# A two-layer attention trunk: x resident behind the norm weights, and the distance table moved from VectorE to GpSimd

## The chip, the cores and the metric

The kernel runs on one core of one Trainium2 chip. The metric is the device time of one execution in microseconds (us); lower is better. A core has a matrix engine (TensorE, PE in the profile, with PEld for its weight loads), VectorE (DVE), ScalarE (ACT), GpSimd (POOL) and SyncE (SP), which here issues every DMA. Each engine works through its own queue in order, and waits on semaphores for what others produce. SBUF is the on-chip memory with 128 partitions; matmuls accumulate in banks of PSUM.

## The reference, cut to what matters

The model has two layers over 256 tokens of width 2048, in float32. Layer A is latent attention with 16 heads, layer B differential attention with 8 heads and a distance penalty.

```python
def rms_norm(x, gain):
    y = xf * lax.rsqrt(jnp.mean(xf * xf, axis=-1, keepdims=True) + EPS)
    return (y * gain)
...
def mla_layer(x, pos, ...):                        # layer A
    z = rms_norm(x, norm_g) @ w_in
    cq, ckv, k_pe, gate = jnp.split(z, ...)        # 512, 512, 64 and 2048 columns
    q = (rms_norm(cq, q_norm_g) @ w_q_up)...       # then heads, rotary part, softmax with a chunk mask
    return x + (o * jax.nn.silu(gate)) @ w_out
...
def diff_attend(q, k, v, pos, lam):                # layer B
    dist = jnp.abs(pi[:, :, None] - pos[:, None, :])
    sc = sc - slopes * dist
    sc = jnp.where(chunk_allowed(pi, pos), sc, -jnp.inf)
    p = jax.nn.softmax(sc, axis=-1)
    p_diff = p[:, :, 0] - lam * p[:, :, 1]
```

`lam` comes from two dot products of learned vectors: the exponential of the one, less the exponential of the other, plus a constant. `chunk_allowed` lets a token see its own chunk of 64 and all before it.

## The kernel before, in words

**Arithmetic.** Each product is made of three matmuls (`mm3`, lines 122 to 125): both operands are split into a high half, rounded to the matrix engine's format, and a low half, the remainder; high times high, high times low and low times high are summed. The low half of a weight tile (`wlo`) is made on DVE, from the raw tile and the high half (line 119); the high half (`whi`) is a cast on ACT (line 118; the very first piece is cast on DVE).

**Weights.** `stream` (line 105) loads one tile of weights from HBM (`raw`, four buffers) and splits it (`whi` and `wlo`, three buffers each). Every matmul weight of the kernel comes through it. A load of `raw` waits until the tile four back is split; a cast to `whi` waits until PE is done with the tile three back.

**The stage of the change.** x arrives feature-major (`xT`, 16 tiles of 128 features by 256 tokens). Line 163 runs a loop over k = 0 to 15. Step k loads one weight tile of 128 x 1088 (`wz[k]`, for k under 3 split in three pieces, for k = 0 loaded in three as well); scales tile k of x by its norm weight and splits it (`xh` on ACT, line 151, and `xl` on DVE, line 152); and runs 18 matmuls, three for each of three column blocks and two halves of the tokens, into six PSUM banks (`pg`, `pu`, `pa`). x is loaded one tile at a time for k = 0 and 1, then two at a time, through a tag of two buffers (`xs`, line 166). After each load's last step, ACT squares the raw x (lines 185 and 188) and POOL adds the squares up (`sqx`, line 189), for the mean square of each token. The norm weights (`gains_t`) are loaded behind the first piece of weights and the first tile of x (line 169). At k = 7 the positions and some small rows are loaded (lines 194 to 196).

Behind the loop in the program stand the tables (lines 199 to 283): rotary angles, sines and cosines (`ang`, `cs`, `ropc`, `rops`), the chunk mask `maskA`, the distance table `distB` (lines 272 to 275, on DVE: subtract, absolute value, add a very large number where the mask forbids, change the sign), and the two dot products for `lam` (`lamp`, `lams`, lines 279 and 281). Nothing in layer A uses `distB`; layer B reads it once per head (line 675, on POOL) and adds it to the scores. `posrf` and `posf` are the positions as floats, along the free axis and on the partitions.

Then follow the latents (`latents`, line 292: squares on ACT, scaling on DVE, and a reciprocal root on POOL), the heads of layer A with the gate's projection between them, its output projection, and layer B in the same manner.

**Order.** The program is written in the order above, and a scheduler orders each engine's queue by priority (earlier lines first) and readiness as it foresees it. So the table instructions stand between the steps of the loop on DVE, and the exponential of `lams` (line 619) stands on ACT among the casts of the last weight tiles. SP's DMA issues keep the program's order. The tag `junk` has one buffer: `lamp` and the throwaway outputs of the squares share it. The tag `gh` in the pool `big` is a buffer of 16 x 256 floats per partition; its first user before is `goh`, the attention output of layer A.

Of the kernel before, what the change touches and what calls it, by code (L numbers as in the profile page):

```python
# [9 lines left out]
F32 = mybir.dt.float32  # L10
# [3 lines left out]
AF = mybir.ActivationFunctionType  # L14
# [4 lines left out]
P = 128  # L19
# [35 lines left out]
def hybrid_kernel(ctx: ExitStack, tc: tile.TileContext, x, xT, pos, posc, rows, gains, wz, wgA, wqu, wkvu, woA, wB, woB, out):  # L55
# [18 lines left out]

# [1 line left out]
    gains_t = const.tile([P, 2 * KD + 14], F32, tag="gains", name="gains_t")  # L76
# [16 lines left out]

    # keep the tensor engine's clock up while the first operands arrive
    wsrc = const.tile([P, 512], BF16, tag="wsrc", name="wsrc")
# [4 lines left out]

# [1 line left out]
    state = {}  # L102
# [24 lines left out]
    def project(accs, lhs, blocks, w, c0, c1, nk):  # L127
        """accs[b][t] += lhs(k, t) . weights of block b, for the chunks c0..c1 of two contraction tiles each."""
        for c in range(c0, c1):
            ws = [stream(b[c], 2 * w) for b in blocks]  # L130
            for kk in range(2):
                k = 2 * c + kk
                for (hi, lo), acc in zip(ws, accs):
                    for t in range(NT):
                        xh, xl = lhs(k, t)
                        mm3(acc[t], xh, xl, hi[:, kk * w:(kk + 1) * w], lo[:, kk * w:(kk + 1) * w],
                            k == 0, k == nk - 1)
# [7 lines left out]

# [1 line left out]
    xh = big.tile([P, KD, S], F32R, tag="xh", name="xh")  # L147
# [11 lines left out]
    ZB = [(0, 384), (384, 384), (768, 320)]  # L159
    xt = [None]  # L160
    sqx = sm.tile([P, 2 * S], F32, tag="kn", name="sqx", bufs=1)
    XC = [0, 1] + list(range(2, KD + 1, 2))
    for k in range(KD):
        def load_x(k=k):
            n = XC[XC.index(k) + 1] - k
            xs = att.tile([P, n, S], F32, tag="gT", name="xs", padded_shape=[P, 4, S])
            nc.sync.dma_start(xs, xT[:, k:k + n, :])
            if k == 0:
                nc.sync.dma_start(gains_t, gains)
            xt[0] = (k, xs, n)  # L170

        if k in XC and k > 0:
            load_x()
        wh, wl = stream(wz[k], ZW, [c for c, _ in ZB] + [ZW] if k < KCUT else None, load_x if k == 0 else None)
        k0, xs, n = xt[0]
        split_gain(xh[:, k, :], xl[:, k, :], xs[:, k - k0, :], gA_t[:, k:k + 1])
        for b, (c0, w) in enumerate(ZB):
            for t in range(NT):
                sl = slice(t * P, (t + 1) * P)
                mm3(zacc[b][t][:, :w], xh[:, k, sl], xl[:, k, sl], wh[:, c0:c0 + w], wl[:, c0:c0 + w],  # L180
                    k == 0, k == KD - 1)
        if k == k0 + n - 1:
            w = n * S
            if k < 2:
                A.activation(sqx[:, k * S:(k + 1) * S], xs.rearrange("p a b -> p (a b)"), AF.Square)
            else:
                sq = sm.tile([P, w], F32, tag="sg", name="sq", bufs=2)
                A.activation(sq, xs.rearrange("p a b -> p (a b)"), AF.Square)
                G.tensor_tensor(sqx[:, :w], sqx[:, :w], sq, ALU.add)
        if k == KCONST:  # L190
            posc_t = const.tile([P, NT], I32, tag="posc", name="posc_t")
            prow = sm.tile([P, 2, S], I32, tag="e", name="prow", bufs=2)
            rows_t = sm.tile([P, HR + 2 * ROPE + 4 * HD], F32, tag="qn", name="rows_t", bufs=1)
            nc.sync.dma_start(posc_t, posc)
            nc.sync.dma_start(prow[:, 0, :], pos.partition_broadcast(P))
            nc.sync.dma_start(rows_t, rows.partition_broadcast(P))

    # mean square of each row of x, and its root's reciprocal
    r0 = const.tile([P, NT], F32, tag="r0", name="r0")
# [14 lines left out]

# [1 line left out]
    posr_t = prow[:, 0, :]  # L216
# [25 lines left out]
    A.activation(cos_, kk_, AF.Sin)  # L242
    # ropc[q|k]: cosines, rops: signed sines, both times the gain of the element they multiply
    V.tensor_scalar(gqkr_t[:, 1, :], gqkr_t[:, 1, :], math.sqrt(AQK), None, ALU.mult)
# [25 lines left out]
    for t in range(NT):  # L270
        V.tensor_scalar(maskA[:, t, :], chrf, chcf[:, t:t + 1], -MASK, ALU.is_gt, ALU.mult)
        V.tensor_scalar(distB[:, t, :], posrf, posf[:, t:t + 1], None, ALU.subtract)
        V.scalar_tensor_tensor(distB[:, t, :], distB[:, t, :], -1.0, distB[:, t, :], ALU.mult, ALU.max)
    V.scalar_tensor_tensor(distB, maskA, -MASK_DIST / MASK, distB, ALU.mult, ALU.add)
    V.tensor_scalar(distB, distB, -1.0, None, ALU.mult)

    # lambda, on every partition
    lamp = sm.tile([P, 2, HD], F32, tag="junk", name="lamp", bufs=1)
    V.tensor_tensor(lamp, lam_t[:, 0:2, :], lam_t[:, 2:4, :], ALU.mult)
    lams = const.tile([P, 2], F32, tag="lams", name="lams")  # L280
# [3 lines left out]

# [1 line left out]
    m16 = big.tile([P, 2, 2, 4, S], F32R, tag="m16", name="m16")  # L286
# [5 lines left out]
    def latents():  # L292
# [13 lines left out]
        for t in range(NT):  # L306
# [4 lines left out]
            cns.append(cn)  # L311
        # shared rotary key: its square sum, and its rotated form with the gain
        kp = sm.tile([P, NT, ROPE], F32, tag="kp", name="kp", bufs=1)
# [25 lines left out]

# [1 line left out]
    KC = KD // 2  # L341
# [26 lines left out]
    def k_up(hp):  # L368
        """keys, normalised, and values of two heads"""
        ka = pair(psu)  # L370
        project([ka], lat(1), [wkvu[hp]], 512, 0, 2, 4)
        kn = sm.tile([P, NT, 2, NOPE], F32, tag="kn", name="kn", bufs=1)
        rt = sm.tile([P, 2, NT, 2, ROPE], F32, tag="rt", name="rt", bufs=1)
        ss = sm.tile([P, 2, NT, 2], F32, tag="ssq", name="ss")
        f = sm.tile([P, 2, NT, 2], F32, tag="fq", name="fq")
        for t in range(NT):
            k3 = ka[t].rearrange("p (h d) -> p h d", h=2)
            junk = sm.tile([P, 512], F32, tag="junk", name="junk", bufs=1)
            for h in range(2):
                A.activation(junk[:, :NOPE], k3[:, h, :NOPE], AF.Square, accum_out=ss[:, 1, t, h:h + 1])  # L380
        V.tensor_tensor(ss[:, 1], ss[:, 1], bc(sskp, 2), ALU.add)
        rsqrt(f[:, 1].rearrange("p b c -> p (b c)"), ss[:, 1].rearrange("p b c -> p (b c)"))
        vh = att.tile([P, NT, 2, P], F32R, tag="vh", name="vh")
        vl = att.tile([P, NT, 2, P], F32R, tag="vl", name="vl")
        for t in range(NT):
            k3 = ka[t].rearrange("p (h d) -> p h d", h=2)
            V.tensor_tensor(kn[:, t], k3[:, :, :NOPE], bc(f[:, 1, t], NOPE), ALU.mult)
            split(vh[:, t], vl[:, t], k3[:, :, NOPE:])
        for t in range(NT):
            V.tensor_tensor(rt[:, 1, t], krope[:, t, :].unsqueeze(1).broadcast_to([P, 2, ROPE]),  # L390
                            bc(f[:, 1, t], ROPE), ALU.mult)
        state["k", hp] = (kn, rt, ss, f, vh, vl)

    def q_up(hp):
        """queries of two heads, not scaled: their norm enters with the scores"""
        kn, rt, ss, f, vh, vl = state["k", hp]
# [25 lines left out]
    def head_t(hp):  # L422
# [13 lines left out]
        for i in (1, 0):  # L436
            for t in range(NT):
                T.transpose(pt[:, i, t * P:(t + 1) * P], rt[:, i, t].rearrange("p h d -> p (h d)"), ident)
        # each head's rotary rows: q as [hi; lo], k's hi and lo twice over, so that every product has 128 rows
        q2 = att.tile([P, 2, S], F32R, tag="q2", name="q2")  # L440
# [116 lines left out]

# [1 line left out]
    x1 = big.tile([P, NT, D], F32, tag="m16", name="x1")  # L559
# [65 lines left out]

# [1 line left out]
    def qk_b(h, c0, c1):  # L627
# [131 lines left out]

# [1 line left out]
    def finish_b(n, t, c0, c1):  # L761
# [20 lines left out]
def _columns(w, width):  # L782
    """(K, N) -> (N / width, K / 256, 128, 2 * width): blocks of columns in chunks of two row tiles."""
    k, n = w.shape
    a = w.reshape(k // 256, 2, 128, n // width, width).transpose(3, 0, 2, 1, 4)
    return a.reshape(n // width, k // 256, 128, 2 * width)
# [46 lines left out]
```

## Time and profile before

| | us |
|---|---|
| median of three runs (lowest, highest) | 847.49 (846.46, 847.53) |
| span of the profiled execution, first to last instruction | 845.0 |
| what the median has above that span | 2.5 |
| PE busy in the span | 835.9 |
| DVE, ACT, POOL busy | 564.6, 488.0, 86.4 |

No time of the profiled execution other than its span is given. A profile row of a timeline has the start, the duration, the engine, the line of the kernel, the operation, output and inputs, the shape and the number of merged instructions; in brackets stands the idle time of that engine before it, and what ended it. A row of the waits has the instruction that waited, what it waited for, the total, the number of times and the longest. A row of windows has a stretch, its length, and the busy time and number of instructions of PE, PEld, DVE, ACT and POOL, then the granted clock, the DMA share and the rate. The granted clock of TensorE is 1.000 throughout. Shares of the whole span say little about the first 60 us, which hold everything the diff touches; they have to be read there.

### The profile page before, as it was taken

To read this page: it belongs to the slowest core of one execution; us is meant where nothing else is said; L and a number is where in the kernel's file an instruction comes from. 1 tells how busy PE (TensorE), PEld (TensorE's weight loads), DVE (VectorE), ACT (ScalarE), POOL (GpSimd) and SP (SyncE) were. 2 spreads that over 40 slices of the span, in tenths; PEclk is the share of its full clock that TensorE was granted. 3 is DMA by queue.
4 is the path that set the end of the run, shared out by engine and by line. 5 is a ranking of instruction groups with operands and counts; after the bars stand their busy time and mean duration, and the time that the engine had idled before them with its cause. 6 is when DMAs were issued, how large, how long until landed. Compare 5 with 4: busy or idle time off the path is not lost.

```text
span 845.0 us, 11706 instructions
## 1 busy us (share of the span) xinstructions
PE 835.9 (99%) x4187; PEld 714.5 (85%) x4187; DVE 564.6 (67%) x968; ACT 488.0 (58%) x995; POOL 86.4 (10%) x113
## 2 busy tenths in 40 slices
PE   8999999999999999999999999999999999999998
PEld 6988888889888888888888888888888888888886
DVE  6968678788787866555647565565756566565543
ACT  7656687677767656555555465555555564554331
POOL 2300221122202200000010010010001000000000
PEclk9999999999999999999999999999999999999999
DMA  8755544534444645555555555554555555455661
GB/s 268 256 197 162 166 147 146 176 116 162 144 144 149 248 154 180 180 186 177 185 175 174 175 175 175 175 175 150 193 181 175 175 175 171 168 184 198 219 211 70
DMA packets 42954, 148.59 MB, mean 176 GB/s; under 512 B 5008, under 2 KB 6032, under 8 KB 42640
## 3 DMA queue, kind: packets, MB, share of 16 engines
q1 hardware_dynamic: 42896, 147.84, 52.5%
q8 instruction: 33, 0.54, 0.3%
q14 instruction: 25, 0.20, 0.1%
HBM read 145.73 MB, written 2.10 MB: 175 GB/s over the span
## 4 chain that ended last, share of the span: by engine, by line
PE 94%; DVE 3%; DMA 1%; ACT 1%; issue 0%; SPq 0%; POOL 0%; DVEq 0%; ACTq 0%
PE pu L123 14%; PE pu L125 14%; PE pu L124 14%; PE pg L124 13%; PE pg L123 13%; PE pg L125 13%; DVE wlo L119 1%; PE ptb L651 1%; PE ptn L430 1%; PE ptp L484 1%; PE pa L124 1%; DMA raw<-in_wz 1%; PE pa L125 1%; PE pa L123 1%; DVE xl L152 1%; PE ps L462 0%
## 5 line engine op out<-in xcount | busy, mean ns | idle before, releaser
L119 DVE TENSOR_TENSOR wlo<-raw,whi 128x1024 fp32r<-128x1024 f32 (+4 forms) x278 | 328.6, 1191 | 189.8 <-ACT whi L118 189.5
L118 ACT CAST whi<-raw 128x1024 fp32r<-128x1024 f32 (+3 forms) x277 | 282.2, 1025 | 233.6 <-PE pg L125 102.6
L123 PE MATMUL pu<-whi,x1h 128*128 128x512 f32 x256 | 101.3, 396 | 0.0
L123 PE MATMUL pg<-whi,x1h 128*128 128x512 f32 x256 | 100.5, 392 | 0.0
L125 PE MATMUL pu<-whi,x1l 128*128 128x512 f32 x256 | 99.9, 390 | 0.0
L124 PE MATMUL pu<-wlo,x1h 128*128 128x512 f32 x256 | 99.8, 390 | 0.0
L124 PE MATMUL pg<-wlo,x1h 128*128 128x512 f32 x256 | 99.7, 390 | 0.0
L125 PE MATMUL pg<-whi,x1l 128*128 128x512 f32 x256 | 99.7, 389 | 0.0
L125 PEld LDWEIGHTS pu<-whi,x1l 128*128 128x128 f32 x256 | 48.1, 188 | 10.2
L125 PEld LDWEIGHTS pg<-whi,x1l 128*128 128x128 f32 x256 | 48.1, 188 | 10.1
L123 PEld LDWEIGHTS pg<-whi,x1h 128*128 128x128 f32 x256 | 48.1, 188 | 9.5
L124 PEld LDWEIGHTS pg<-wlo,x1h 128*128 128x128 f32 x256 | 48.1, 188 | 9.4
L124 PEld LDWEIGHTS pu<-wlo,x1h 128*128 128x128 f32 x256 | 48.2, 188 | 9.2
L123 PEld LDWEIGHTS pu<-whi,x1h 128*128 128x128 f32 x256 | 48.1, 188 | 9.2
L123 PE MATMUL pg<-whi,xh 128*128 128x512 f32 (+1 forms) x128 | 49.8, 391 | 1.9 <-ACT whi L118 1.3
L124 PE MATMUL pg<-wlo,xh 128*128 128x512 f32 (+1 forms) x128 | 48.7, 381 | 1.9 <-DVE wlo L119 1.9
L123 PE MATMUL pg<-whi,goh 128*128 128x512 f32 x128 | 50.5, 395 | 0.0
L123 PE MATMUL pu<-whi,goh 128*128 128x512 f32 x128 | 50.1, 392 | 0.0
L124 PE MATMUL pg<-wlo,goh 128*128 128x512 f32 x128 | 49.9, 390 | 0.0
L125 PE MATMUL pg<-whi,gol 128*128 128x512 f32 x128 | 49.9, 390 | 0.0
L124 PE MATMUL pu<-wlo,goh 128*128 128x512 f32 x128 | 49.9, 390 | 0.0
L125 PE MATMUL pu<-whi,gol 128*128 128x512 f32 x128 | 49.9, 389 | 0.0
(246 smaller groups left out, 1551.1 us busy)
## 6 DMA issues: line engine op xcount, KB each, us to landing
raw<-in_wB SPq DMA_DIRECT2D x128, 512.0 KB, 3.2
raw<-in_wgA SPq DMA_DIRECT2D x32, 512.0 KB, 3.5
raw<-in_woA SPq DMA_DIRECT2D x32, 512.0 KB, 3.3
raw<-in_woB SPq DMA_DIRECT2D x32, 512.0 KB, 3.2
raw<-in_wkvu SPq DMA_DIRECT2D x16, 512.0 KB, 4.3
raw<-in_wz SPq DMA_DIRECT2D x15, 544.0 KB, 5.7
raw<-in_wqu SPq DMA_DIRECT2D x16, 384.0 KB, 3.1
x<-in_x SPq DMA_DIRECT2D x1, 2048.0 KB, 10.0
```

The source lines that it names most:

```text
L118: (V.tensor_copy if after_first and a == 0 else A.copy)(hi[:, a:b], raw[:, a:b])
L119: V.tensor_tensor(lo[:, a:b], raw[:, a:b], f32(hi[:, a:b]), ALU.subtract)
L123: T.matmul(o, shi, mhi, start=start, stop=False)
L124: T.matmul(o, shi, mlo, start=False, stop=False)
L125: T.matmul(o, slo, mhi, start=False, stop=stop)
L152: V.scalar_tensor_tensor(lo, src, g, f32(hi), ALU.mult, ALU.subtract)
L430: T.transpose(pt[:, h, t * P:(t + 1) * P], src[:, t, h, :NOPE], ident)
L484: T.transpose(pt[:, c, t * P:(t + 1) * P], e[:, t, c * P:(c + 1) * P], ident)
L651: T.transpose(pt[:, m, t * P:(t + 1) * P], qk[:, t, 2 * i + m, :], ident)
```

## The change

Two parts; comments and blank lines aside, nothing else is edited.

The first keeps the whole of `xT` in one buffer, 16 KiB in each partition, in the tag `gh`. Each load writes its own part of it, at the same places in the program as before, so that no load waits for an earlier part to be used. The load of the norm weights is issued first of all.

The second makes `distB` and `lamp` on GpSimd: minus the absolute distance as min(d, 0) - max(d, 0) with a helper tile `ahead`, then the mask's share (`far`) added. That is nine instructions on POOL in place of seven on DVE. The sum of `lamp` (`lams`) stays on DVE.

```diff
-            xs = att.tile([P, n, S], F32, tag="gT", name="xs", padded_shape=[P, 4, S])
-            nc.sync.dma_start(xs, xT[:, k:k + n, :])
-            if k == 0:
-                nc.sync.dma_start(gains_t, gains)
...
+    xs = big.tile([P, KD, S], F32, tag="gh", name="xs")
...
+    def load_x(k):
+        n = XC[XC.index(k) + 1] - k
+        nc.sync.dma_start(xs[:, k:k + n, :], xT[:, k:k + n, :])
+
+    nc.sync.dma_start(gains_t, gains)
     for k in range(KD):
...
+        split_gain(xh[:, k, :], xl[:, k, :], xs[:, k, :], gA_t[:, k:k + 1])
...
     for t in range(NT):
         V.tensor_scalar(maskA[:, t, :], chrf, chcf[:, t:t + 1], -MASK, ALU.is_gt, ALU.mult)
-        V.tensor_scalar(distB[:, t, :], posrf, posf[:, t:t + 1], None, ALU.subtract)
-        V.scalar_tensor_tensor(distB[:, t, :], distB[:, t, :], -1.0, distB[:, t, :], ALU.mult, ALU.max)
-    V.scalar_tensor_tensor(distB, maskA, -MASK_DIST / MASK, distB, ALU.mult, ALU.add)
-    V.tensor_scalar(distB, distB, -1.0, None, ALU.mult)
+        ahead = sm.tile([P, S], F32, tag="junk", name="ahead", bufs=1)
+        G.tensor_scalar(ahead, posrf, posf[:, t:t + 1], 0.0, ALU.subtract, ALU.max)
+        G.tensor_scalar(distB[:, t, :], posrf, posf[:, t:t + 1], 0.0, ALU.subtract, ALU.min)
+        G.tensor_tensor(distB[:, t, :], distB[:, t, :], ahead, ALU.subtract)
+    far = sm.tile([P, NT * S], F32, tag="junk", name="far", bufs=1)
+    G.tensor_scalar(far, maskA.rearrange("p a b -> p (a b)"), MASK_DIST / MASK, 0.0, ALU.mult, ALU.add)
+    G.tensor_tensor(distB.rearrange("p a b -> p (a b)"), distB.rearrange("p a b -> p (a b)"), far, ALU.add)
...
-    V.tensor_tensor(lamp, lam_t[:, 0:2, :], lam_t[:, 2:4, :], ALU.mult)
+    G.tensor_tensor(lamp, lam_t[:, 0:2, :], lam_t[:, 2:4, :], ALU.mult)
```

More of the change, by code (lines that the diff above doesn't have):

```diff
@@ L159, in hybrid_kernel @@
     ZB = [(0, 384), (384, 384), (768, 320)]
-    xt = [None]
+    xs = big.tile([P, KD, S], F32, tag="gh", name="xs")
     sqx = sm.tile([P, 2 * S], F32, tag="kn", name="sqx", bufs=1)
     XC = [0, 1] + list(range(2, KD + 1, 2))
+    def load_x(k):
+        n = XC[XC.index(k) + 1] - k
+        nc.sync.dma_start(xs[:, k:k + n, :], xT[:, k:k + n, :])
+    nc.sync.dma_start(gains_t, gains)
     for k in range(KD):
-        def load_x(k=k):
-            n = XC[XC.index(k) + 1] - k
-            xs = att.tile([P, n, S], F32, tag="gT", name="xs", padded_shape=[P, 4, S])
-            nc.sync.dma_start(xs, xT[:, k:k + n, :])
-            if k == 0:
-                nc.sync.dma_start(gains_t, gains)
-            xt[0] = (k, xs, n)
         if k in XC and k > 0:
[L173 to L176, printed above, removed]
+            load_x(k)
+        wh, wl = stream(wz[k], ZW, [c for c, _ in ZB] + [ZW] if k < KCUT else None, (lambda: load_x(0)) if k == 0 else None)
+        split_gain(xh[:, k, :], xl[:, k, :], xs[:, k, :], gA_t[:, k:k + 1])
         for b, (c0, w) in enumerate(ZB):
@@ L181, in hybrid_kernel @@
                     k == 0, k == KD - 1)
-        if k == k0 + n - 1:
-            w = n * S
+        if k + 1 in XC:
+            k0 = XC[XC.index(k + 1) - 1]
+            src = xs[:, k0:k + 1, :].rearrange("p a b -> p (a b)")
+            w = (k + 1 - k0) * S
             if k < 2:
-                A.activation(sqx[:, k * S:(k + 1) * S], xs.rearrange("p a b -> p (a b)"), AF.Square)
+                A.activation(sqx[:, k * S:(k + 1) * S], src, AF.Square)
             else:
                 sq = sm.tile([P, w], F32, tag="sg", name="sq", bufs=2)
-                A.activation(sq, xs.rearrange("p a b -> p (a b)"), AF.Square)
+                A.activation(sq, src, AF.Square)
                 G.tensor_tensor(sqx[:, :w], sqx[:, :w], sq, ALU.add)
```

## The prediction

> **What bounds the kernel now.** I read the page's first two parts, then the waits of TensorE in the first 70 us, then the timelines of DVE, ACT, POOL and SP there. On the page:
>
> ```profile
> PE 835.9 (99%) x4187; PEld 714.5 (85%) x4187; DVE 564.6 (67%) x968; ACT 488.0 (58%) x995; POOL 86.4 (10%) x113
> ```
>
> TensorE (PE) is busy 99% of 845.0 us, so the change can only touch the few microseconds in which PE waits. The waits up to 70 us, which hold all that the diff touches, are:
>
> ```profile
> PE pg L124 <- DVE wlo L119: 1.9, 2, 1.2
> PE pg L123 <- ACT whi L118: 1.3, 1, 1.3
> PE pg L123 <- ACT xh L151: 0.7, 1, 0.7
> ```
>
> That is 3.9 us, 0.46% of the span, and the prize can't be larger. The timeline of PE places them (start, duration, engine, line, tile, and in brackets the idle time before and what ended it):
>
> ```profile
> 9.50 0.62 PE L123 MATMUL pg<-whi,xh 128*128 128x384 f32 x2 [1.26 <-ACT whi L118]
> 13.99 0.44 PE L124 MATMUL pg<-wlo,xh 128*128 128x384 f32 x1 [0.72 <-DVE wlo L119]
> 43.86 0.34 PE L123 MATMUL pg<-whi,xh 128*128 128x384 f32 x1
> 45.38 0.44 PE L124 MATMUL pg<-wlo,xh 128*128 128x384 f32 x1 [1.18 <-DVE wlo L119]
> 45.66 0.33 PE L125 MATMUL pg<-whi,xl 128*128 128x384 f32 x1
> 45.83 0.34 PE L123 MATMUL pg<-whi,xh 128*128 128x384 f32 x1
> ```
>
> The first two belong to the start (k = 1 and k = 2 of the sixteen steps that multiply x by `wz`), the last to step 12. The start is the business of the first half of the change, step 12 of the second. At step 12, PE waits for the low half of the weights, `wlo`, and DVE made it late. I number that instruction by its step, wlo12; it is the first row here, and the others show what DVE did since it was last level with its suppliers:
>
> ```profile
> 44.04 1.28 DVE L119 TENSOR_TENSOR wlo<-raw,whi 128x1088 fp32r<-128x1088 f32 x1
> 24.18 1.29 DVE L119 TENSOR_TENSOR wlo<-raw,whi 128x1088 fp32r<-128x1088 f32 x1 [0.23 <-ACT whi L118]
> 32.00:40.00 8.00, 8.00 (x50) 8.00 (x49) 8.00 (x21) 5.83 (x11) 3.32 (x2) 1.00 0.76 239
> ```
>
> At 24.18 DVE still waited for ACT, so it was level. From then on it never idles (the window 32 to 40: 8.00 of 8.00 us in the third number), and 20 us later PE stands still for it. So in this stretch each microsecond added to DVE's queue is one of PE's, and each taken away is one saved until the wait is used up.
>
> **The start: x and the norm weights.** Now x goes through two small buffers, and SP issues its queue in the order of the program. So a load of x that waits for a buffer holds up the weights behind it:
>
> ```profile
> SPq L116 <- DVE wlo L119: 33.8, 16, 6.4
> SPq L167 <- DVE xl L152: 9.1, 6, 2.5
> 3.52 0.43 SPq L116 DMA_DIRECT2D raw<-in_wz  x1
> 5.48 0.33 SPq L167 DMA_DIRECT2D xs<-in_xT  x1
> 5.86 0.91 SPq L116 DMA_DIRECT2D raw<-in_wz  x2
> ```
>
> With one resident buffer there is nothing to wait for: x for k = 2 goes out at about 4.0 instead of 5.48, the weights of k = 2 and 3 from about 4.4 instead of 5.86, 1.5 us earlier. Most of the 9.1 us isn't worth anything, because the weight loads behind the later x loads wait for their own buffers too (33.8 us of SP's waits are for `wlo`). Putting the norm weights ahead moves `raw` and x of k = 0 by one issue each (0.47 us in this queue) and lets ACT start k = 0 sooner; PE then runs into the load of the weights of k = 1, which is seventh in the queue before and after. So I cost the reordering at nothing; its cover is the 1.26 us wait at 9.50, and without it one issue, 0.47 us, could be lost.
>
> What the earlier x buys shows on ACT and DVE:
>
> ```profile
> 10.72 0.91 ACT L151 ACTIVATE xh<-xs,gains_t 128x256 fp32r<-128x256 f32 x2 [0.50 <-DMA xs<-in_xT]
> 11.54 0.62 ACT L188 ACTIVATE sq<-xs 128x512 f32<-128x512 f32 x1
> 12.27 1.29 ACT L118 CAST whi<-raw 128x384 fp32r<-128x384 f32 x3
> 12.24 1.28 POOL L189 TENSOR_TENSOR sqx<-sqx,sq 128x512 f32<-128x512 f32 x1 [10.95 <-ACT sq L188]
> 12.81 3.32 DVE L119 TENSOR_TENSOR wlo<-raw,whi 128x384 fp32r<-128x384 f32 x4 [0.66 <-ACT whi L118]
> ```
>
> ACT waits 0.50 us for x and, after the square, 0.11 (12.16 to 12.27) for the weights. Both go, 0.6 us. POOL's add moves with them and still stands in front of the first low half of k = 2, so PE's wait at 13.99 shrinks by 0.6 and isn't gone. The ends: all of the wait (0.72, and 0.28 that PE idled just before it), 1.0, if the cast comes ahead of the square; or 0.4 lost, if more loads in flight, or the norm weights ahead, bring the weights of k = 1 later. I take a gain of 0.6, from ACT's rows.
>
> **The distance table.** DVE loses these (minimum, median, maximum in ns; the last row is the sort of POOL instruction that takes over):
>
> ```profile
> L272 DVE TENSOR_SCALAR distB<-rowf,posf x2: 341/342/344, 29.0 to 34.8; 128x256 f32<-128x256 f32 x2
> L273 DVE SCALAR_TENSOR_TENSOR distB<-distB x2: 414/415/416, 29.4 to 42.8; 128x256 f32<-128x256 f32 x2
> L274 DVE SCALAR_TENSOR_TENSOR distB<-maskA,distB x1: 677/677/677, 43.4 to 43.4; 128x512 f32<-128x512 f32 x1
> L279 DVE TENSOR_TENSOR lamp<-rows_t x1: 412/412/412, 35.1 to 35.1; 128x256 f32<-128x256 f32 x1
> L675 POOL TENSOR_SCALAR bias<-distB x8: 620/1457/1533, 267.6 to 647.9; 128x512 f32<-128x512 f32 x8
> ```
>
> Ahead of wlo12 that is 2 x 0.34 + 2 x 0.41 + 0.68 + 0.41 = 2.6 us; consecutive DVE instructions overlap by some 0.08, so six of them free 2.1 us of the queue. (L275 goes too, but it stands behind wlo12.)
>
> POOL gains nine instructions: four tensor_scalar on 256 elements, two tensor_tensor on 256, `far` (tensor_scalar on 512), an add on 512 and `lamp` (tensor_tensor on 256). Two rows price the tensor_tensor forms:
>
> ```profile
> L416 POOL TENSOR_TENSOR rt<-rt,r x8: 739/741/1586, 100.1 to 285.1; 128x256 f32<-128x256 f32 x8
> L189 POOL TENSOR_TENSOR sqx<-sqx,sq x7: 1282/1426/2436, 12.2 to 40.6; 128x512 f32<-128x512 f32 x7
> ```
>
> 256 elements take 0.74, 512 take 1.28. A tensor_scalar on 512 takes 0.62 undisturbed; on 256 it lies between half of that and all of it, and I take 0.40. Together 4 x 0.40 + 2 x 0.74 + 0.62 + 1.28 + 0.74 = 5.7 us. POOL has the time (3.32 us busy in the 8 us above). The question is whether DVE runs on meanwhile. It doesn't:
>
> ```profile
> 9.48 1.43 DVE L119 TENSOR_TENSOR wlo<-raw,whi 128x384 fp32r<-128x384 f32 x3 [1.41 <-ACT whi L118]
> 26.09 0.29 DVE L267 CAST rowf<-prow 128x256 f32<-128x256 int32 x1
> 26.21 1.43 POOL L189 TENSOR_TENSOR sqx<-sqx,sq 128x512 f32<-128x512 f32 x1 [4.69 <-ACT sq L188]
> 26.39 1.53 DVE L152 SCALAR_TENSOR_TENSOR xl<-xs,gains_t,xh 128x256 fp32r<-128x256 f32 x1
> 27.95 0.47 DVE L152 SCALAR_TENSOR_TENSOR xl<-xs,gains_t,xh 128x256 fp32r<-128x256 f32 x1
> ```
>
> The same DVE instruction takes 1.53 beside POOL's add and 0.47 without it; it ends 0.28 after POOL (27.64 to 27.92). POOL's add of 1.28 costs DVE 1.06. `wlo` suffers the same way: three short ones and a long one would have taken 1.43 and 1.28 less the overlap of 0.08, so 2.6, and took 3.32 from 12.81. So moving work to POOL doesn't take it out of DVE's way.
>
> How much do nine cost? If 0.22 of each is free (1.28 less 1.06), 5.7 less 9 x 0.22 = 3.7 us. If the free part is a share (1.06 of 1.28, 83%), 4.7. If nothing is free, 5.7. If they all fall where DVE doesn't want what POOL holds, 0; a gain below that is excluded, since POOL's instructions can't speed DVE up. I take 3.7: the add's row is the nearest, and a fixed start and end per instruction is what it shows. They come in time to count: the last of their first inputs (`posrf`, the cast at 26.09) exists at 26.4, and 5.7 us of POOL fit well before 44.
>
> The Trainium skill (SBUF — State Buffer, section "Who interferes with whom") has the rule that speaks against the change: DVE's second port pair is shared with GpSimd, and whichever instruction comes first holds it "for the whole instruction". The row gives 1.06 of 1.28, a little less. By the rule to the letter the term is 5.7, the second rival's time; by the row 3.7.
>
> Queues that gain a wait: `lams` (L281, DVE) now waits for POOL's last new instruction, and behind it on DVE stand wlo12 and the rest; ACT's exponential waits for `lams`, and behind that stand two casts of weights:
>
> ```profile
> 43.12 0.41 DVE L281 TENSOR_REDUCE lams<-lamp 128x2 f32<-128x256 f32 x1
> 43.56 0.20 ACT L619 ACTIVATE lams<-lams 128x2 f32<-128x2 f32 x1 [1.84 <-DVE lams L281]
> 43.67 2.08 ACT L118 CAST whi<-raw 128x1088 fp32r<-128x1088 f32 x2
> 46.98 1.29 DVE L119 TENSOR_TENSOR wlo<-raw,whi 128x1088 fp32r<-128x1088 f32 x1
> ```
>
> ACT waits there already, 1.84 us. Its next cast ends at 44.7 and DVE uses it at 46.98, so 2.2 us of cover; POOL's chain should be over by about 40. I cost this at nothing. POOL's next work after the sixteen steps comes at 58:
>
> ```profile
> 58.19 0.72 POOL L92 TENSOR_TENSOR r<-msx,nhalf 128x2 f32<-128x2 f32 x1 [16.09 <-DVE msx L208]
> ```
>
> It has idled 16 us by then, so it isn't held up. The users of `distB` start at 267.6.
>
> **The sum.** Against the profiled span of 845.0: start -0.6; freed on DVE -2.1; lost by DVE to POOL +3.7; together +1.0, so 846.0, PE's wait at step 12 growing from 1.2 to about 2.8. The median of the runs, 847.49, stands 2.5 above the span; the same shift gives 848.5. A change within 0.2%, 1.7 us, can't be told from none here, so "the same" is 845.8 to 849.2.
>
> **The rivals.** (1) Relief: the new work falls into moments when DVE wants nothing that POOL holds, or the order on DVE comes out so that the low halves go first. Then step 12's wait is gone (1.35: the matmul after the one at 43.86 should have started 0.17 later, as the rows at 45.66 and 45.83 do, not 1.52), and with the start -1.9: 845.6. For it: POOL is idle most of the stretch. Against: both the long weights and the short x instruction were held. It decides where DVE loses less than 2.1 - 1.35 = 0.8 us. (2) The port is held for the whole of each instruction, or DVE stands in order behind `lams` while POOL finishes: 5.7 - 2.1 - 0.6 = +3.0, 850.5. It turns the sign beyond doubt where DVE loses more than 2.1 + 0.6 + 1.7 = 4.4. For it: the nine follow one another, and each DVE instruction between them may meet a fresh one. (3) The start gains nothing because the loads share the same DMA engines: 3.7 - 2.1 = +1.6, 849.1, or above with the 0.4. (4) Loss and relief cancel: about 847.
>
> **How the numbers follow.** My forecast has 0.46 (0.36 of it within 0.2%, 0.10 above, since its own range, DVE losing 3.2 to 4.7, is 848.0 to 849.5), relief 0.19, full hold 0.23, no gain at the start 0.07 (half of it above), cancelling 0.05. Faster 0.19; same 0.36 + 0.03 + 0.05 = 0.44; slower 0.10 + 0.23 + 0.04 = 0.37. The low end is the relief with 0.3 more at the start, 845.3; the high end the full hold with the start's gain lost, 851.0.
>
> **What would show it.** Right: `xs` issues back to back with no wait on `xl`; PE's wait at k = 2 about 0.6 shorter, at k = 1 unchanged; nine POOL instructions between about 25 and 42, beside them L152 and L119 rows of 0.7 to 2 us; the wait of PE on `wlo` at step 11 or 12 at 2 to 3 us; nothing new after 60 us. Wrong: undisturbed L152 rows of 0.47 beside the new POOL instructions, or no wait at step 12 (relief); ACT idle for `lams` by more than 4 us (the queue); `raw` of k = 1 landing after 9.2 (the start).

## The result, and the profile after

| | before | after |
|---|---|---|
| median of five runs, us (lowest, highest) | 847.49 (846.46, 847.55) | 853.64 (852.78, 854.29) |
| ratio of the times (95% interval) | | 1.0076 (1.0064, 1.0088) |
| span of the profiled execution, us | 845.0 | 851.0 |

The change makes the kernel 6.2 us slower, 0.76%. That is 5.1 us above the forecast and 2.6 above the end of the range. From the page of the changed kernel:

```profile
PE 838.1 (98%) x4187; PEld 716.5 (84%) x4187; DVE 562.0 (66%) x961; ACT 490.7 (58%) x997; POOL 95.0 (11%) x122
```

POOL has its nine instructions more and DVE seven fewer, as the diff says. TensorE's waits of the changed kernel up to 75 us (its warm-up and a row of 0.3 us are left out); the last row is from 75 to 320 us, where the kernel before has no wait on `vl`:

```profile
PE pg L124 <- DVE wlo L119: 5.7, 2, 4.8
PE pg L123 <- ACT whi L118: 0.6, 1, 0.6
...
PE pu L123 <- DVE vl L156: 1.0, 1, 1.0
```

One wait has grown to 4.8 us, where the longest was 1.3. The timeline of PE in the changed kernel (start, duration, and in brackets the idle time and what ended it):

```profile
9.22 0.61 PE L123 MATMUL pg<-whi,xh 128*128 128x384 f32 x2 [0.63 <-ACT whi L118]
13.75 0.44 PE L124 MATMUL pg<-wlo,xh 128*128 128x384 f32 x1 [0.91 <-DVE wlo L119]
...
34.52 0.34 PE L123 MATMUL pg<-whi,xh 128*128 128x384 f32 x1
39.69 0.69 PE L124 MATMUL pg<-wlo,xh 128*128 128x384 f32 x1 [4.84 <-DVE wlo L119]
40.18 0.52 PE L125 MATMUL pg<-whi,xl 128*128 128x384 f32 x1
40.50 0.52 PE L123 MATMUL pg<-whi,xh 128*128 128x384 f32 x1
...
44.02 0.34 PE L123 MATMUL pg<-whi,xh 128*128 128x384 f32 x1
...
121.24 0.41 PE L123 MATMUL pu<-whi,m 128*128 128x384 f32 x1 [1.00 <-DVE vl L156]
```

The wait isn't at step 12 but at step 9, and behind it the matmuls start 0.32 us apart where 0.17 is usual. The windows of the changed kernel show why; the granted clock is the third number from the right:

```profile
40.00:41.00 1.00, 1.00 (x4) 1.00 (x4) 0.93 (x5) 0.42 (x3) 0.00 (x0) 0.50 0.53 65
41.00:42.00 1.00, 1.00 (x5) 1.00 (x4) 0.93 (x5) 1.00 (x3) 0.00 (x0) 0.50 0.72 270
42.00:43.00 1.00, 1.00 (x5) 1.00 (x5) 1.00 (x5) 1.00 (x4) 0.00 (x0) 0.57 0.99 392
```

After standing still, TensorE was granted half its clock for some three microseconds. The seventeen matmuls from the end of the wait, 39.69, to the next step, 44.02, took 4.33 us. The kernel before took 2.91 us for the same ones behind its wait, from 45.38 to the next step, which starts here:

```profile
48.29 0.34 PE L123 MATMUL pg<-whi,xh 128*128 128x384 f32 x1
```

So some 1.4 us are lost on top of the wait. What DVE was doing, in its timeline of the changed kernel:

```profile
26.66 0.61 DVE L152 SCALAR_TENSOR_TENSOR xl<-xs,gains_t,xh 128x256 fp32r<-128x256 f32 x1
...
29.33 1.28 DVE L119 TENSOR_TENSOR wlo<-raw,whi 128x1088 fp32r<-128x1088 f32 x1
30.53 0.76 DVE L234 SCALAR_TENSOR_TENSOR ang<-kh__596,ang 128x64 f32<-128x64 f32 x1
37.30 0.42 DVE L285 TENSOR_REDUCE lams<-lamp 128x2 f32<-128x256 f32 x1 [6.00 <-POOL lamp L283]
37.63 2.00 DVE L119 TENSOR_TENSOR wlo<-raw,whi 128x1088 fp32r<-128x1088 f32 x1
```

DVE, which never idled in this stretch before, stood 6.00 us for `lamp`, with the low half of step 9 directly behind it. In the kernel before `lams` stood at 43.12, shortly ahead of the low half of step 12; in the new program the scheduler put it ahead of step 9's. (The first row is used further down.) POOL's timeline of the changed kernel shows what `lamp` waited for:

```profile
26.24 1.44 POOL L274 TENSOR_SCALAR ahead<-rowf,posf 128x256 f32<-128x256 f32 x1 [5.09 <-DVE kk__595 L228]
27.66 2.33 POOL L275 TENSOR_SCALAR distB<-rowf,posf 128x256 f32<-128x256 f32 x2
29.97 1.25 POOL L276 TENSOR_TENSOR distB<-distB,ahead 128x256 f32<-128x256 f32 x1
31.17 1.29 POOL L189 TENSOR_TENSOR sqx<-sqx,sq 128x512 f32<-128x512 f32 x1
32.44 1.15 POOL L274 TENSOR_SCALAR ahead<-rowf,posf 128x256 f32<-128x256 f32 x1
33.67 0.74 POOL L276 TENSOR_TENSOR distB<-distB,ahead 128x256 f32<-128x256 f32 x1
34.50 0.62 POOL L278 TENSOR_SCALAR far<-maskA 128x512 f32<-128x512 f32 x1
35.20 1.26 POOL L279 TENSOR_TENSOR distB<-distB,far 128x512 f32<-128x512 f32 x1
36.54 0.72 POOL L283 TENSOR_TENSOR lamp<-rows_t 128x256 f32<-128x256 f32 x1
37.22 1.26 POOL L189 TENSOR_TENSOR sqx<-sqx,sq 128x512 f32<-128x512 f32 x1
```

`lamp` needs nothing of the table, but it is last of the nine on an engine that works in order. The nine take 1.44 + 2.33 + 1.25 + 1.15 + 0.74 + 0.62 + 1.26 + 0.72 = 9.5 us, not 5.7. (The expectations of two runs below put the new work at 8.7.) ACT's exponential then stood 5.10 us for `lams`:

```profile
37.75 0.20 ACT L623 ACTIVATE lams<-lams 128x2 f32<-128x2 f32 x1 [5.10 <-DVE lams L285]
```

The account, from the profiled executions: the wait 4.84 - 1.18 = +3.7, the halved clock +1.4, the new wait for `vl` +1.0, the first 14 us -0.24 (13.75 against 13.99): 5.9 of the 6.0 us by which the span grew. The rest is spread over small gaps and was not assigned. The profiled execution is the shortest of the five, 852.78 us, with a mean granted clock of 0.998. Three of the others had 0.995 and took 853.64 to 854.29 us, so the clock's share in the median is probably larger; there is no trace of them.

### The profile page after: what moved, and what is told of

Read it like the earlier page. It is cut to its first block, busy times and chain, and to the rows that moved or that the text cites. A ratio compares the mean times of both kernels' runs of the same rounds, so it can differ in the third digit from the quotient of the medians.

```text
span 851.0 us, 11698 instructions
## 1 busy us (share of the span) xinstructions
PE 838.1 (98%) x4187; PEld 716.5 (84%) x4187; DVE 562.0 (66%) x961; ACT 490.7 (58%) x997; POOL 95.0 (11%) x122
## 4 chain that ended last, share of the span: by engine, by line
PE 93%; DVE 2%; POOL 1%; ACT 1%; DMA 1%; issue 0%; SPq 0%; DVEq 0%; ACTq 0%; POOLq 0%
PE pu L123 14%; PE pu L125 13%; PE pu L124 13%; PE pg L124 13%; PE pg L125 13%; PE pg L123 13%; DVE wlo L119 1%; PE pa L124 1%; PE pa L125 1%; PE ptb L655 1%; PE ptp L488 1%; PE pa L123 1%; DMA xs<-in_xT 1%; PE ptn L434 1%; ACT whi L118 1%; PE psb L125 0%
```

## The experiments

Two theories stood against each other: the loss is the queue's (DVE waits in order behind POOL, and the clock halves for it), or it is the port's (DVE can't run beside POOL). Each ratio is against the kernel before on the same chip; that kernel's medians were 847.23, 846.79 and 847.10 us in the three sessions.

**The parts alone.** `e3_x_only` is the kernel before with the diff's first part, `e4_table_only` with its second.

> The first part alone: x in one resident buffer behind the norm weights, all tables on DVE as before. Theories Q and P agree: PE's wait at k = 2 ends 0.2 to 0.6 us earlier and nothing else changes, 846.9 to 847.3. Theory X (the first part is the cause): 852 or more.

> The second part alone: x loaded through two small buffers as before, distance table and lamp on GpSimd. Theories Q and P: 853 to 854.5, with DVE waiting about 6 us for lamp (Q) or with stretched DVE rows and no such wait (P). Theory X: 847 to 848.

Measured: x alone 846.94 us, ratio 0.9995 (0.9985 to 1.0004), which can't be told from no change; the table alone 853.24, ratio 1.0069 (1.0053 to 1.0084). The second has the same two waits as the whole change, for `wlo` 4.8 us at the longest and for `vl` 1.0. So the loss is the table part's.

**The wait for `lamp`.** `e1_lamp_dve` makes `lamp` on DVE again and leaves the table on POOL; `e2_lamp_first` leaves `lamp` on POOL and puts it ahead of the table.

```diff
e1:
-    G.tensor_tensor(lamp, lam_t[:, 0:2, :], lam_t[:, 2:4, :], ALU.mult)
+    V.tensor_tensor(lamp, lam_t[:, 0:2, :], lam_t[:, 2:4, :], ALU.mult)
e2, ahead of the loop over t that makes the table:
+    lamp = sm.tile([P, 2, HD], F32, tag="junk", name="lamp", bufs=1)
+    G.tensor_tensor(lamp, lam_t[:, 0:2, :], lam_t[:, 2:4, :], ALU.mult)
```

> The changed kernel with one edit: lamp is made on DVE again, the distance table stays on GpSimd. In the changed kernel DVE stands 6.00 us for lamp behind GpSimd's chain and PE 4.84 us behind DVE. Theory Q (the in-order wait for lamp is the cost): that wait goes, PE's wait near step 9 goes with it, 846.5 to 848. Theory P (GpSimd's instructions hold DVE's port, the forecast's term): lamp is only 0.72 of 8.7 us of new GpSimd work, so the time stays at 852 to 853.5.

> The changed kernel with one edit: lamp stays on GpSimd but is written ahead of the distance table, so that it stands first in GpSimd's chain. The work on each engine is the same as in the changed kernel. Theory Q: lams finds lamp ready or waits under 1.5 us, 846.5 to 848.5. Theory P: the same GpSimd work in the same stretch, 852 to 854.

Measured: e1 853.34, ratio 1.0065 (1.0051 to 1.0080); e2 851.71, ratio 1.0043 (1.0028 to 1.0059). In e1 the wait hadn't gone at all. DVE's timeline of e1:

```profile
37.76 1.47 DVE L283 TENSOR_TENSOR lamp<-rows_t 128x256 f32<-128x256 f32 x1 [5.21 <-POOL distB L279]
```

DVE now waits for POOL's add of `far` instead. `lamp`, `ahead` and `far` share the one buffer of the tag `junk`, and `lamp` may not write there until `far` has been read: the same queue, through a buffer. e1 therefore tells nothing of the port.

In e2 the wait for `lamp` is gone, but 3.6 us (by the ratio) to 4.5 us (851.71 against that session's 847.23) are still lost, which is in neither theory's range. Timelines of POOL and DVE in e2:

```profile
37.89 5.14 POOL L189 TENSOR_TENSOR sqx<-sqx,sq 128x512 f32<-128x512 f32 x3
39.00 4.18 DVE L254 SCALAR_TENSOR_TENSOR rops<-rows_t,cs 128x32 f32<-128x32 f32 x8
```

Three adds of squares, which arrive one by one in the kernel before, stand piled up behind the table and now run in a row. Beside them eight small DVE instructions take 4.18 us; undisturbed (in e11, below) they take 0.90. PE waits 3.4 us for low halves in e2, in four pieces. This looks like the port of the prediction, at work through adds that the kernel had all along; `e6_pool_late` below gives the comparison that shows it.

**The same with a buffer of its own.** `e5_lamp_own` is e1 with `lamp` in the tag `r2`, so that nothing on DVE waits for POOL.

```diff
-    lamp = sm.tile([P, 2, HD], F32, tag="junk", name="lamp", bufs=1)
-    G.tensor_tensor(lamp, lam_t[:, 0:2, :], lam_t[:, 2:4, :], ALU.mult)
+    lamp = sm.tile([P, 2, HD], F32, tag="r2", name="lamp", bufs=1)
+    V.tensor_tensor(lamp, lam_t[:, 0:2, :], lam_t[:, 2:4, :], ALU.mult)
```

> The run with lamp on DVE still stood 5.21 us, now for the release of the one buffer that lamp shares with GpSimd's helper tiles. Here lamp is on DVE in a buffer of its own, so DVE waits for nothing of GpSimd's chain. Theory Q alone (the wait in DVE's queue is the whole cost): 847 to 848. Theory Q and P together (the wait, or else the hold on DVE's port and the squares queued up behind the chain on GpSimd, as in the run with lamp first): no wait for GpSimd on DVE, but stretched DVE rows, 850 to 852.

Measured: 850.61, ratio 1.0044 (1.0030 to 1.0057). Timelines of POOL and DVE in e5:

```profile
38.13 4.97 POOL L189 TENSOR_TENSOR sqx<-sqx,sq 128x512 f32<-128x512 f32 x3
38.30 2.27 DVE L119 TENSOR_TENSOR wlo<-raw,whi 128x1088 fp32r<-128x1088 f32 x1
40.49 3.07 DVE L254 SCALAR_TENSOR_TENSOR rops<-rows_t,cs 128x32 f32<-128x32 f32 x8
```

The longest waits of PE in e5, up to 75 us and behind it:

```profile
PE pg L124 <- DVE wlo L119: 3.1, 2, 2.2
PE pu L123 <- DVE vl L156: 1.0, 1, 1.0
```

And one of e5's windows:

```profile
42.00:43.00 1.00, 1.00 (x5) 1.00 (x4) 1.00 (x1) 0.00 (x0) 1.00 (x1) 0.50 0.88 344
```

With no wait of DVE for POOL the table still costs 3.7 us (0.0044 of 847), as the two theories together expected. In the profiled execution PE waits 1.0 longer than before in one piece (2.2 against 1.2), loses some 1.5 to three microseconds of halved clock (4.46 us from the end of the wait, 40.62, to the next step, 45.08, against the 2.91 above), and has the late wait for `vl`, 1.0. As time the clock's part isn't shown: three of the five executions had a mean granted clock of 1.000 and took 850.08, 850.17 and 850.98 us, the two with 0.998 took 850.61 and 850.77. So the theory that the queue is all of it has fallen: part of what it cost is lost to the held port instead once it is gone.

**The price of the operation.** POOL's tensor_scalar on 256 elements took 1.1 to 1.4 us, and `far`, on 512, 0.62. `e8_immediate` replaces the operand `posf` by the constant 0 (its table leaves out the query's position); `e11_mult_add` also makes the operations a multiplication by 1 and an addition of 0 (its table holds no distances). The output of both leaves that much of the decay out.

```diff
-        G.tensor_scalar(ahead, posrf, posf[:, t:t + 1], 0.0, ALU.subtract, ALU.max)
e8:
+        G.tensor_scalar(ahead, posrf, 0.0, 0.0, ALU.subtract, ALU.max)
e11:
+        G.tensor_scalar(ahead, posrf, 1.0, 0.0, ALU.mult, ALU.add)
```

> The changed kernel with the four GpSimd instructions that subtract a token's position taking the constant 0 in place of the per-partition operand; the distance table is therefore without the query's position. With DVE idle that form took 1.15 us on 256 elements, against 0.62 for 512 with constants. If the operand makes the difference, each falls to about 0.35, the chain from 8.7 to about 5.5 us, DVE's wait for lamp from 6.0 to about 3, PE's from 4.8 to about 1.7, and the clock isn't lowered: 848.5 to 850. If it doesn't, 853 to 854.

> The changed kernel with the operations of the four tensor_scalar instructions on 256 elements put to multiply and add with constants, on the same tiles and engine; the table then holds no distances, and the output leaves the decay by distance out. Theory (subtract with max or min is what takes 1.1 us, since the multiply-and-add on 512 elements took 0.62): about 0.35 each, POOL's chain ends 2.5 to 3 us earlier, VectorE's wait for lamp falls from 6.0 to about 3 us, PE's for wlo from 4.8 to 1.7 or 2, and the time is 848.5 to 850.5. Rival (256 elements of a stretched row map cost 1.1 us whatever the operation): no change, 853 to 854.

Measured: e8 853.37, ratio 1.0077 (1.0065 to 1.0090); e11 851.32, ratio 1.0046 (1.0033 to 1.0060). One row of POOL's timeline from e8, at a place where DVE was idle, and then one from e11, beside small DVE instructions:

```profile
33.17 1.06 POOL L274 TENSOR_SCALAR ahead<-rowf 128x256 f32<-128x256 f32 x1
```

```profile
30.68 0.41 POOL L274 TENSOR_SCALAR ahead<-rowf 128x256 f32<-128x256 f32 x1
...
41.25 0.90 DVE L254 SCALAR_TENSOR_TENSOR rops<-rows_t,cs 128x32 f32<-128x32 f32 x8
38.27 0.44 PE L124 MATMUL pg<-wlo,xh 128*128 128x384 f32 x1 [2.61 <-DVE wlo L119]
```

The operand hardly matters (1.15 with it, 1.06 without), the operation does: 0.41 with multiply and add although DVE was running. (The second fence also has the eight small DVE instructions with no POOL work beside them.) In e11's profiled execution PE's wait is 2.61, 2.2 us shorter than in the changed kernel, and the clock stays at 1.00. That execution is the shortest of the five, 850.24 us. The other four had a mean granted clock of 0.997 or 0.998 and took 851.21 to 851.63 us. The median is 1.9 us (medians, each less its session's before) to 2.5 us (ratios) better than the changed kernel's, and 0.8 us above the expected range. `lamp` ended 1.4 us earlier (35.85 for 37.26), not 2.5 to 3, since with DVE running on longer POOL was the one that was held. From e11's timelines:

```profile
31.17 1.78 POOL L276 TENSOR_TENSOR distB<-distB,ahead 128x256 f32<-128x256 f32 x1
31.08 1.28 DVE L119 TENSOR_TENSOR wlo<-raw,whi 128x1088 fp32r<-128x1088 f32 x1
```

POOL's instruction, which takes 0.74 us in the changed kernel, isn't over until 32.95. Less its 0.74 that is 32.21, about when the low half, which came 0.09 earlier, was done (32.36).

**The table out of the way.** `e6_pool_late` makes the table on POOL behind the latents, `e7_dve_late` on DVE at the same place; both have x resident and `lamp` on DVE. The new tile `posl` = 0 x (a sum of squares made there) + `posf` holds the table back until then.

```diff
+    posl = const.tile([P, NT], F32, tag="posl", name="posl")
+    V.scalar_tensor_tensor(posl, sskp, 0.0, posf, ALU.mult, ALU.add)
+    for t in range(NT):
e6:
+        ahead = sm.tile([P, S], F32, tag="rt", name="ahead", bufs=1)
+        G.tensor_scalar(ahead, posrf, posl[:, t:t + 1], 0.0, ALU.subtract, ALU.max)
...
e7:
+        V.tensor_scalar(distB[:, t, :], posrf, posl[:, t:t + 1], None, ALU.subtract)
...
```

> The resident x, lamp on DVE as before the change, and the distance table on GpSimd but made to wait for the latents (its positions take a term 0 x sskp), so that it runs after 67 us, out of the stage where PE hangs on DVE. Q and P both: PE's wait at step 12 goes (1.35 us), nothing replaces it, 845.3 to 846.5. If GpSimd's table costs wherever it stands: 848 or more.

> The same late place for the distance table, but on DVE with the four instructions per table of before the change; nothing of the table is on GpSimd. Q and P: 845.3 to 846.5, equal to the late table on GpSimd within 0.5 us, because after 67 us neither engine sets PE's pace. If DVE is short there too: 847 or more.

Measured: e6 847.04, ratio 1.0001 (0.9992 to 1.0009); e7 847.10, ratio 1.0003 (0.9994 to 1.0012). In e6 POOL's first instruction of the table, at 67.64, takes 2.30 us, and PE has no wait near the table; so what it costs early is a matter of its place. It also settles what e5 left open. From `lams` on, e5 and e6 have the same twenty instructions in the same order on DVE, up to the eight small ones, and no idle time among them. With the table beside them (e5) these take 11.80 us, from 31.76 to 43.56; with the table late (e6) 6.48, from 32.01 to 38.49. The last two rows of that stretch in e6, to be read against e5's 2.27 and 3.07:

```profile
36.39 1.28 DVE L119 TENSOR_TENSOR wlo<-raw,whi 128x1088 fp32r<-128x1088 f32 x1
37.59 0.90 DVE L254 SCALAR_TENSOR_TENSOR rops<-rows_t,cs 128x32 f32<-128x32 f32 x8
```

So POOL's work stretched DVE by 5.3 us in e5, without any wait in order. The wait of step 12 is gone in e6 and e7, yet nothing is won, and both stand above the expected 845.3 to 846.5. PE's waits of e7, up to 75 us and then to 320 (its warm-up left out):

```profile
PE pg L123 <- DVE wlo L119: 0.8, 1, 0.8
PE pu L123 <- DVE vl L156: 1.0, 1, 1.0
```

The late wait takes it back. DVE's timeline there, first of the kernel before, then of e7:

```profile
114.56 0.75 DVE L156 TENSOR_TENSOR vl<-pu,vh 128x256 fp32r<-128x256 f32 x2
...
115.42 0.48 DVE L468 CUSTOM_DVE_ANT_0 e<-ps,maskA,fq 128x256 f32<-128x256 f32 x1
```

```profile
113.42 0.48 DVE L464 CUSTOM_DVE_ANT_0 e<-ps,maskA,fq 128x256 f32<-128x256 f32 x1
...
114.63 0.75 DVE L156 TENSOR_TENSOR vl<-pu,vh 128x256 fp32r<-128x256 f32 x2
```

Before, the low half of v (`vl`, in `k_up`) runs ahead of three row maxima; in e7, and in every kernel here whose table isn't early on DVE, behind them. Nothing of the table is near: given another program, the scheduler chose another order here too, some 45 us and more behind the table.

**That order put right.** In `k_up` the split of v is written ahead of `kn`: `e9_v_first` does it to e7, `e10_after_v_first` to the changed kernel, `e12_before_v_first` to the kernel before.

```diff
+        for t in range(NT):
+            split(vh[:, t], vl[:, t], ka[t].rearrange("p (h d) -> p h d", h=2)[:, :, NOPE:])
         for t in range(NT):
             k3 = ka[t].rearrange("p (h d) -> p h d", h=2)
             V.tensor_tensor(kn[:, t], k3[:, :, :NOPE], bc(f[:, 1, t], NOPE), ALU.mult)
-            split(vh[:, t], vl[:, t], k3[:, :, NOPE:])
```

> This is the kernel with x resident and the table on VectorE after the latents (847.10, the same time as before), with one more edit: in layer A the two instructions that split v are written ahead of the one that makes kn. Theory (the start gives back half a microsecond and the wait of step 12 goes; what cancels them is the 1.0 us wait of PE for vl in the last window of the score stage): with vl made ahead of the row maxima the wait for vl L156 goes, and the time is 845.5 to 846.2. Rival (the wait is the price of VectorE being busy there, and something else of the same size comes late in its place): another wait of 0.8 to 1.2 us in the same place, 846.8 to 847.4.

> The changed kernel with the split of v written ahead of kn, and nothing else. Theory (the late wait is worth 1.0 to 1.1 us of the changed kernel's 6.2 and is independent of the wait at 37 us): PE's wait for vl is gone, that for wlo stays at 4.8, and the time is 852.4 to 852.8. Rival (the late wait is only the shadow of the earlier one): no change, 853.3 to 853.8.

> Control: the kernel before with the split of v written ahead of kn. In the kernel before vl already ran ahead of the row maxima and PE did not wait for it. Theory: no change, 846.8 to 847.4. Rival (the edit is worth something by itself, whatever the table): over 0.5 us faster, 846.3 or less.

Measured: e9 845.96, ratio 0.9984 (0.9976 to 0.9993); e10 852.82, ratio 1.0060 (1.0047 to 1.0073); e12 847.24, ratio 1.0002 (0.9991 to 1.0012). The wait for `vl` is in none of the three. The edit is worth 1.1 us to e7, by the medians, with intervals that don't overlap, and nothing where the order was right already. To the changed kernel it is worth 0.4 to 1.4 (by the medians less their sessions' before, or by the ratios), with intervals that do overlap; e10's profiled execution, in which the halved clock lasted from 39 to 45, is no shorter than the changed kernel's (851.1). So for the changed kernel the 1.0 us of this wait is shown as a wait and only weakly as time. The only waits of PE that the trace of e9 lists up to 320 us, its warm-up apart, are of 1.4, 0.4 and 0.4 us, in the first 15.

e9 beats both kernels, the one before by 0.16% (0.07% to 0.24%), 1.4 us. It has x resident; whether it needs that wasn't tried.

## Why the prediction was wrong

**What bounds the kernel** was right: PE's waits in the first 60 us, and DVE as the engine that makes them. The direction was right too, but partly by luck: the sum was positive by the port alone, and that isn't what the changed kernel mostly paid.

**The step that failed** is "Queues that gain a wait ... I cost this at nothing". It took 2.2 us of cover from ACT's next cast and set the end of POOL's chain, about 40, against the place of `lams` before, 43.12. POOL's chain was even over sooner, at 37.3. But the order on DVE wasn't kept: `lams` came directly ahead of the low half of step 9, and DVE was there 6.00 us ahead of POOL. PE's wait went to 4.84, at step 9, and the clock halved. e2 and e5, which take that wait away, win back 2.8 and 2.7 us by the ratios (1.7 and 2.3 by the medians, each less its session's before). That isn't the whole miss: without the wait, e5 still loses 3.7 us where the sum had +1.0, by the mis-sized chain, the stretched DVE and the wait for `vl` below. No run kept `lams` at its old place behind the new chain, so what the forecast was worth there stays open. The mechanism did stand in the second rival ("DVE stands in order behind `lams`"), but it was priced as if it could cost no more than POOL's nine instructions less what was freed, 850.5, with no clock in it.

**A term mis-sized**: POOL's nine instructions, 5.7 us forecast, 9.5 measured. The four tensor_scalar were taken at 0.40 from a row of another operation; e11 shows 0.41 for multiply and add, e8 and the changed kernel 1.06 to 1.44 for subtract with max or min. The other five took 4.6 against 4.1. The sum also left out what the chain does to POOL's own queue: three adds of squares came late and in a row, and stretched DVE (5.14 us of them in e2, 4.97 in e5).

**The port** was right as a mechanism and is not what the changed kernel mostly paid: DVE stood for `lamp` during most of POOL's chain, so it had little to lose there. What POOL held was wanted by the 2.00 us of `wlo` at 37.63, 0.72 over its 1.28, beside the add at 37.22. In e5, where DVE runs on, the port is the main loss: 5.3 us on DVE, against the 3.7 of the prediction. The Trainium skill (SBUF — State Buffer, section "Who interferes with whom") lets whichever came first keep the shared pair for the whole instruction. It says so of VectorE's two-port modes; of an instruction with two inputs in SBUF it says that it contends. With the adds the trace nearly agrees (5.14 us of them stretched eight DVE instructions from 0.90 to 4.18). With POOL's tensor_scalar it doesn't: beside the 1.44 us one at 26.24 the changed kernel's `xl` took 0.61, 0.14 more than 0.47.

**DVE freed, -2.1**: right as a mechanism, as e7 shows (the wait of step 12 goes, 1.2 us of it being all there was to win there), and buried in the changed kernel under the 6.00 us wait. Its size isn't shown by itself, since the order on DVE changed with it.

**The start, -0.6**: wrong. x for k = 2 was issued at 4.00 with no wait on `xl`, as forecast, and ACT still waited 0.54 for it. PE's wait at k = 2 grew from 0.72 to 0.91 and the one at k = 1 fell from 1.26 to 0.63, the other way round than forecast. The 0.24 that came of it isn't more than the scatter: the matmul at 13.99 before and 13.75 after stands at 14.09 in e3 and 14.20 in e9, which have x resident too. The DMA rows of the first 14 us, before and then after (KB each, then median us from issue to landing):

```profile
raw<-in_wz SPq DMA_DIRECT2D x5, 544.0 KB, 6.4
xs<-in_xT SPq DMA_DIRECT2D x3, 256.0 KB, 5.4
```

```profile
raw<-in_wz SPq DMA_DIRECT2D x5, 544.0 KB, 7.3
xs<-in_xT SPq DMA_DIRECT2D x3, 256.0 KB, 6.5
```

By these medians, what was issued earlier took a microsecond longer. That fits the third rival, at 0.07: the DMA engines were 76% busy in these 14 us before and 79% after. No run tests it by itself.

**"Nothing new after 60 us"**: wrong, by the 1.0 us for `vl`; e9, e10 and e12 show that it goes with the order on DVE.

Of the marks named ahead for being wrong, "ACT idle for `lams` by more than 4 us (the queue)" came true: 5.10 us. "No wait at step 12 (relief)" came true by the letter, but the wait had moved to step 9, so it was no relief.

## What to carry to other kernels

When work moves to another engine, ask first which instruction of the old engine will wait for it in order, through data or through a shared buffer, and price that wait by the whole chain ahead of it on the new engine. Where a scheduler makes the order, the order of before is no evidence of where the waiting instruction will stand, and edits can cost time far from where they are made. A matrix engine that stands a few microseconds can pay again in its clock, here some 1.4 us behind a wait of 4.84.

## What the runs showed of the hardware that wasn't expected

- On POOL a tensor_scalar on 128 x 256 took 0.41 us with multiply and add (e11) and 1.06 with subtract and max (e8, DVE idle); with a tile for the second operand, in the changed kernel, it took 1.15.
- The halved clock doesn't follow from the length of the wait before it alone. In the profiled executions it came after 4.84 us (changed kernel), 2.18 (e5) and 2.05 (e2), and not after 2.61 (e11, granted 1.00 from 36 to 44). Executions of one kernel differ too: e11's mean granted clock was 1.000 once and 0.997 or 0.998 four times, and the kernel before had four executions at 0.998 (849.09 to 849.49 us) in the last session, where the others had 0.999 or 1.000. The Trainium skill (TensorE: Matmul & The Clock Gate, section "Part 1: The HAM clock gate") has the clock halved after at least one idle window of about 3.4 us, and the windows run free of the kernel. That it differs between executions of one kernel fits; that some 2 us of standing did it doesn't.
